# A rotary embedding on one core: every other row added on TensorE, VectorE makes a sine product in single batches, loads issued 18 rows behind

## The chip, the cores and the metric

The kernel runs on one core of a Trainium2 chip. A core has five engines, each with its own stream of instructions: TensorE (PE; its weight loads are shown as PEld), VectorE (DVE), ScalarE (ACT), GpSimd (POOL) and SyncE (SP). Transfers between the device's memory and the core's on-chip memory are done by sixteen DMA engines; they are issued here by ACT (loads) and SP (stores). The metric is the device time of one execution in microseconds, as a median over runs; less is better.

## What is computed

```python
batch, seq, dim = (16, 512, 1024); num_heads = 16; head_dim = 64
x = x.reshape(batch, seq, num_heads, head_dim)
x1, x2 = (x[..., :half_dim], x[..., half_dim:])
cos = cos[None, :, None, :]
sin = sin[None, :, None, :]
rotated = np.concatenate([x1 * cos - x2 * sin, x1 * sin + x2 * cos], axis=-1)
```

All in float32. 33.6 MB are read and 33.6 MB written. For each element there are two products (one with the cosine; one of the other half of its head with the sine, negative for the first half) and one add.

## The kernel before

**Tiles and rows.** The 128 partitions hold the sequence. Batches 0, 1, 14 and 15 are loaded one at a time (R1 = 4 positions of the sequence per partition), the others in six pairs (R2 = 8 positions). That makes ten tiles: two singles, six pairs, two singles. A "row" is one position per partition, 128 x 1024 floats (0.52 MB); there are NU = 64 rows, numbered through. `x_sb` is a ring of RING = 40 rows, worked on in place: the result of a row is written over its input and stored from there.

**Work on a row u.**

- a sine product into `t2_sb` (a ring of NT2 = 6 buffers, shown as t_sb in the profile): POOL (L257), or, where V2[u] is true, DVE (L286), with the halves of each head swapped as it reads and a signed sine table
- a cosine product into `t1_ps` (a ring of NT1 = 3 buffers in the accumulation memory, t_ps in the profile): always DVE (L293)
- the add. Where PE2[u] is false, DVE adds the two and writes `x_sb` (L304, `comb`). Where it is true, TensorE multiplies the sine product with an identity matrix and accumulates on the cosine product (L224, two 512-wide matmuls, seen as four records), and ACT copies the sum to `x_sb` (L191)

PE2 is true for rows 1, 3 and 6 of every eight, except in the first and the last batch: 21 rows. V2 is true for row 3 of every pair: six rows. Thus POOL makes 58 sine products.

**Order.** DVE goes through the rows: `mul(u)`, then `comb(u - 1)` if that row is not PE's. `mul(u)` waits until row u - 3 is added, by ACT's copy or DVE's add, because it takes over its buffer. POOL, and DVE where it makes the sine product, wait until row u - 6 is added. PE waits for both products of its row. ACT's stream holds the copies in order of rows and the loads among them.

**Tables.** The cosine and sine tables are loaded once, 64 KB each. ACT makes signed sine tables for POOL (L182 to L187). For its own sine product of pairs DVE makes a small signed table `v_ps` (L271, L272: 0.19 us each) just before row 8.

**Loads and stores.** The first six loads (tiles 0 to 5, 40 rows) are issued at once. Each of the other four takes over a place in the ring. It stands in ACT's stream behind the copies up to a certain row and waits there until the store of the rows whose place it takes has landed:

```python
later.setdefault((b * R1 - RING) // R2 * R2 + R2 - 1 + LAG, []).append(t)
```

With LAG = 10 the seventh load stands after row 17, the eighth after row 25, the ninth and tenth after row 33. SP issues the store of a tile when all its rows are added (L161).

Of the kernel before, what the change touches and what calls it, by code (L numbers as in the profile page):

```python
# [6 lines left out]
def bass_split_heads_rope_kernel(  # L7
# [18 lines left out]
    HD = dim // H  # L26
    HALF = HD // 2
    P = 128
    R1 = seq // P
    R2 = 2 * R1  # L30
# [4 lines left out]
    mult = mybir.AluOpType.mult  # L35
# [5 lines left out]
    tiles = [(b, R1 if b in singles else R2) for b in range(batch) if b in singles or b % 2 == 0]  # L41
    NT = len(tiles)
    RING = 5 * R2

    rows = [(t, r) for t, (_, n) in enumerate(tiles) for r in range(n)]
    NU = len(rows)
    EARLY = (NU - RING) // R2


    V_ROW = 3  # L50
    PE2 = [R1 <= u < NU - R1 and u % R2 in (1, 3, 6) for u in range(NU)]
    V2 = [tiles[t][1] == R2 and r == V_ROW for t, r in rows]

    def count(flags):
        return [sum(flags[: u + 1]) for u in range(NU)]

    n_pool = count([not v for v in V2])
    n_pe = count(PE2)
    n_comb = count([not a for a in PE2])

    NT1 = 3
    NT2 = 6
    BANK = 512
    EH = H * HD // BANK
    LEAD = 1
    LAG = 10

    with ExitStack() as stack:
        x_sb = stack.enter_context(nc.sbuf_tensor([P, RING, H, 2, HALF], fp32))
        t2_sb = stack.enter_context(nc.sbuf_tensor([P, NT2, H, 2, HALF], fp32))  # L70
        stage = stack.enter_context(nc.sbuf_tensor([P, 2, R1 * HALF], fp32))
# [5 lines left out]
        tab_ps = stack.enter_context(nc.psum_tensor([P, BANK], fp32))  # L77
        pair_ps = stack.enter_context(nc.psum_tensor([P, 2, 2, R1, HALF], fp32))
# [5 lines left out]
        sem_sin = stack.enter_context(nc.semaphore("sin"))  # L84
        sem_c = stack.enter_context(nc.semaphore("ctab"))
# [10 lines left out]
        sem_a = stack.enter_context(nc.semaphore("act"))  # L96

        c1_ps = tab_ps[:, 0:R1 * HALF].rearrange("p (r d) -> p r d", d=HALF)
        v_ps = tab_ps[:, R1 * HALF:R1 * HALF + HD].rearrange("p (t d) -> p t d", d=HALF)

        def c_of(t, r):
            return c1_ps[:, r, :] if tiles[t][1] == R1 else pair_ps[:, r // R1, 0, r % R1, :]
# [19 lines left out]
        def where(u):  # L122
            t, r = rows[u]
            return t, r, u % RING

        def swapped(k):
            return x_sb[:, k, :, ::-1, :]

        def over_heads(table):
            return table[:, None, :, :].broadcast_to([P, H, 2, HALF])  # L130
# [8 lines left out]
        def wait_t2_free(eng, u):  # L139

            if u >= NT2:
                v = u - NT2
                if PE2[v]:
                    eng.wait_ge(sem_e, n_pe[v])
                else:
                    eng.wait_ge(sem_v, n_comb[v])
# [17 lines left out]
        def on_scalar(ae):  # L164
            later = {}
            for t, (b, n) in enumerate(tiles):
                if b * R1 + n <= RING:
                    load(ae, t)
                else:

                    later.setdefault((b * R1 - RING) // R2 * R2 + R2 - 1 + LAG, []).append(t)
                if t == 0:
# [15 lines left out]
            for u in range(NU):  # L188
                if PE2[u]:
                    ae.wait_ge(sem_e, n_pe[u])  # L190
# [6 lines left out]
        def on_tensor(pe):  # L197
# [17 lines left out]
            for u in range(NU):  # L215
                if not PE2[u]:
                    continue
                pe.wait_ge(sem_m, u + 1)

                if not V2[u]:  # L220
                    pe.wait_ge(sem_p, n_pool[u])
# [12 lines left out]
        def on_gpsimd(pl):  # L234
# [11 lines left out]
            for u in range(NU):  # L246
                if V2[u]:
                    continue
# [12 lines left out]
        def on_vector(ve):  # L261
            ve.memset(zero[:], 0.0).then_inc(sem_z, 1)  # L262
            ve.wait_ge(sem_cos, 16)
            ve.tensor_copy(c1_ps, stage[:, 0, :].rearrange("s (r d) -> s r d", d=HALF)).then_inc(sem_c, 1)  # L264
            ve.wait_ge(sem_c, 1)
            ve.wait_ge(sem_w, NT1 * EH)

            def pair_tables():
                ve.wait_ge(sem_s, 2)
                row = pair_ps[:, V_ROW // R1, 1, V_ROW % R1, :]  # L270
                ve.tensor_scalar_mul(v_ps[:, 0, :], row, -1.0).then_inc(sem_c, 1)  # L271
                ve.tensor_copy(v_ps[:, 1, :], row).then_inc(sem_c, 1)  # L272

            first_v = V2.index(True)

            def mul(u):
                t, r, k = where(u)
                if r == 0:
                    ve.wait_ge(sem_in[t], 16)
                if (t, r) == (2, 0):  # L280
                    pair_tables()
                if u == first_v:
                    ve.wait_ge(sem_c, 3)
                if V2[u]:
                    wait_t2_free(ve, u)
                    ve.tensor_tensor(t2_sb[:, u % NT2, :, :, :], swapped(k), over_heads(v_ps), mult)  # L286
                if u >= NT1:
                    v = u - NT1
                    if PE2[v]:
                        ve.wait_ge(sem_a, n_pe[v])  # L290
                    else:
                        ve.wait_ge(sem_v, n_comb[v])
                ve.tensor_tensor(  # L293
                    t1_ps[:, u % NT1, :].rearrange("p (h d) -> p h d", d=HALF),
                    x_sb[:, k, :, :, :].rearrange("p h t d -> p (h t) d"),
                    c_of(t, r)[:, None, :].broadcast_to([P, 2 * H, HALF]),
                    mult,
                ).then_inc(sem_m, 1)

            def comb(u):  # L300
                t, r, k = where(u)
                ve.wait_ge(sem_m, u + 1)
                ve.wait_ge(sem_p, n_pool[u])  # L303
                ve.tensor_tensor(  # L304
                    xs[:, k, :],
                    t1_ps[:, u % NT1, :],
                    t2_sb[:, u % NT2, :, :, :].rearrange("p h t d -> p (h t d)"),
                    add,
                ).then_inc(sem_v, 1)

            for u in range(NU + LEAD):
                if u < NU:
                    mul(u)
                if u >= LEAD and not PE2[u - LEAD]:
                    comb(u - LEAD)
# [3 lines left out]
        on_gpsimd(nc.gpsimd)  # L319
        on_tensor(nc.tensor)  # L320
        on_vector(nc.vector)


# [31 lines left out]
```

## Time and profile before

| | |
|---|---|
| median of 3 runs | 161.54 us (161.3 to 161.56) |
| span of the profiled execution, first to last instruction | 160.3 us |
| POOL busy | 134.9 us (84%), 64 instructions |
| DVE busy | 130.3 us (81%), 117 instructions |
| PE busy | 72.8 us (45%), 94 instructions |
| ACT busy | 24.4 us (15%), 27 instructions |
| DMA | 67.26 MB, mean 419 GB/s over the span |
| load issues (seventh to tenth) | 53.6, 73.6, 93.1, 93.4 us |
| store issues, first and last | 20.5, 151.7 us |

Busy time is the time in which an engine executes; issuing a DMA and waiting are not in it. The profiled execution's own device time is not listed apart from its span; the median of the runs is 1.2 us above that span. A row of forty digits shows busy tenths in forty slices of 4.0 us, 9 meaning 90% or more.

### The profile page before, as it was taken

How to read it: one execution, taken by the hardware profiler on the slowest of the kernel's cores; microseconds unless marked ns; L12 is line 12 of the kernel's file. 1: busy time of each engine (PE TensorE's matmuls, PEld its weight loads, DVE VectorE, ACT ScalarE, POOL GpSimd, SP SyncE). 2: the span in 40 equal slices, each digit the busy share in tenths (PEclk: the TensorE clock that was granted, in tenths of full speed). 3: DMA queues.
4: the chain of work that ended last, by engine and by line, in shares of the span. 5: the costliest groups of instructions: out<-in, count | busy, mean ns of one | idle time of the engine just before them, and what ended most of it. 6: DMA issues, size and time to landing. Idle time of an engine off the chain costs nothing.

```text
span 160.3 us, 522 instructions
## 1 busy us (share of the span) xinstructions
PE 72.8 (45%) x94; PEld 24.0 (15%) x94; DVE 130.3 (81%) x117; ACT 24.4 (15%) x27; POOL 134.9 (84%) x64
## 2 busy tenths in 40 slices
PE   6050004478357936660847105489458435850000
PEld 1020002022202211210221002022202111220000
DVE  0069998599989999996999709899889999999500
ACT  0420000203120222022012010201220402040000
POOL 1059999999999999999999999699999999289400
PEclk9955555557755587689687965555555977699555
DMA  5999999999999999999999999999999999999896
GB/s 147 409 441 474 409 450 409 425 429 429 446 429 458 417 411 466 409 433 401 450 433 425 425 409 458 409 433 433 411 429 462 441 417 401 450 441 441 376 450 294
DMA packets 3170, 67.26 MB, mean 419 GB/s; under 512 B 352, under 2 KB 608, under 8 KB 608
## 3 DMA queue, kind: packets, MB, share of 16 engines
q10 hardware_dynamic: 1728, 33.69, 49.6%
q1 hardware_dynamic: 1440, 33.56, 48.9%
q14 instruction: 2, 0.02, 0.0%
HBM read 33.69 MB, written 33.55 MB: 419 GB/s over the span
## 4 chain that ended last, share of the span: by engine, by line
DMA 60%; POOL 13%; DVE 8%; PE 7%; issue 3%; ACT 2%; ACTq 1%; DVEq 0%
DMA x_sb<-in_x_dram 41%; DMA out_dram<-x_sb 18%; POOL t_sb L257 13%; PE t_ps L224 7%; DVE t_ps L293 5%; DVE x_sb L304 3%; ACT x_sb L191 2%; ACTq L153 1%; ACTq L174 1%; DVE t_sb L286 0%; DVEq L303 0%
## 5 line engine op out<-in xcount | busy, mean ns | idle before, releaser
L257 POOL TENSOR_TENSOR t_sb<-x_sb,s_sb 128x1024 f32<-128x1024 f32 x58 | 134.2, 2346 | 14.8 <-ACT s_sb L183 8.5
L224 PE MATMUL t_ps<-t_sb,ident 128*128 128x512 f32 x84 | 68.0, 957 | 63.0 <-DVE t_ps L293 39.2
L293 DVE TENSOR_TENSOR t_ps<-x_sb,pair_ps 128x1024 f32<-128x1024 f32 x48 | 57.7, 1223 | 9.9 <-ACT x_sb L191 9.8
L304 DVE TENSOR_TENSOR x_sb<-t_ps,t_sb 128x1024 f32<-128x1024 f32 x43 | 52.4, 1218 | 2.6 <-POOL t_sb L257 2.6
L224 PEld LDWEIGHTS t_ps<-t_sb,ident 128*128 128x128 f32 x84 | 22.1, 290 | 108.9 <-DVE t_ps L293 74.6
L191 ACT ACTIVATE x_sb<-t_ps 128x1024 f32<-128x1024 f32 x21 | 21.5, 1023 | 109.9 <-PE t_ps L224 96.9
L293 DVE TENSOR_TENSOR t_ps<-x_sb,tab_ps 128x1024 f32<-128x1024 f32 x16 | 19.3, 1222 | 0.1
L286 DVE TENSOR_TENSOR t_sb<-x_sb,tab_ps 128x1024 f32<-128x1024 f32 x6 | 7.3, 1213 | 0.0
L264 DVE COPY tab_ps<-stage 128x128 f32<-128x128 f32 x1 | 0.3, 294 | 7.8 <-DMA stage<-in_cos_dram 7.8
L208 PE MATMUL pair_ps<-stage,pick 128*128 128x256 f32 x4 | 2.0, 667 | 5.4 <-DMA stage<-in_sin_dram 5.4
L201 PE MATMUL t_ps<-zero 128*128 128x512 bf16 x6 | 2.7, 627 | 1.3 <-DVE zero L262 1.3
L208 PEld LDWEIGHTS pair_ps<-stage,pick 128*128 128x128 f32 x4 | 1.2, 324 | 6.4 <-issue 6.3
L177 ACT ACT_TABLE_LOAD x1 | 1.3, 1283 | 5.5 <-issue 5.5
L201 PEld LDWEIGHTS t_ps<-zero 128*128 128x128 bf16 x6 | 0.7, 136 | 2.4 <-DVE zero L262 1.2
L262 DVE MEMSET zero<- 128x256 uint32 x1 | 0.3, 272 | 0.9 <-PEq L337 0.9
L186 ACT ACTIVATE s_sb<-pair_ps 128x256 f32<-128x256 f32 x1 | 0.4, 383 | 1.7 <-PE pair_ps L208 1.7
L182 ACT ACTIVATE s_sb<-stage 128x128 f32<-128x128 f32 x1 | 0.3, 309 | 2.1 <-DMA stage<-in_sin_dram 2.1
L235 POOL MEMSET ident<- 128x128 f32 x1 | 0.2, 204 | 0.3 <-POOLq L337 0.3
L177 ACT ACTIVATE pick<-ident 128x256 f32<-128x256 f32 x1 | 0.4, 416 | 0.0
L187 ACT ACTIVATE s_sb<-pair_ps 128x256 f32<-128x256 f32 x1 | 0.4, 379 | 0.0
L237 POOL TENSOR_SCALAR_AFFINE_SELECT ident<-ident 128x128 f32<-128x128 f32 x1 | 0.3, 292 | 0.1
L337 POOL MEMSET const-float32-0.0<- 128x1 f32 x1 | 0.1, 98 | 0.3 <-issue 0.3
(6 smaller groups left out, 1.0 us busy)
## 6 DMA issues: line engine op xcount, KB each, us to landing
x_sb<-in_x_dram ACTq DMA_DIRECT2D x6, 4096.0 KB, 38.0
out_dram<-x_sb SPq DMA_DIRECT2D x6, 4096.0 KB, 25.0
x_sb<-in_x_dram ACTq DMA_DIRECT2D x4, 2048.0 KB, 22.6
out_dram<-x_sb SPq DMA_DIRECT2D x4, 2048.0 KB, 15.2
stage<-in_cos_dram ACTq DMA_DIRECT2D x1, 64.0 KB, 7.8
stage<-in_sin_dram ACTq DMA_DIRECT2D x1, 64.0 KB, 7.5
```

Of the source, the lines that this page charges most:

```text
L153: eng.dma_start(in_sbuf(t), in_dram(x1, x2, t)).then_inc(sem_in[t], 16)
L174: ae.dma_start(stage[:, i, :], table.rearrange("(s r) d -> s (r d)", r=R1)).then_inc(sem, 16)
L177: ae.activation(pick[:], ident[:].rearrange("q (s k) -> q k s", k=2)[:, :, :, None].broadcast_to([P, 2, P // 2, 2]), COPY).then_inc(sem_g, 1)
L186: ae.activation(s2[:, :, :, 0, :], pair_ps[:, :, 1, :, :], COPY, scale=-1.0)
L191: ae.activation(xs[:, u % RING, :], t1_ps[:, u % NT1, :], COPY).then_inc(sem_a, 1)
L201: pe.matmul(t1_ps[:, k, b * BANK:(b + 1) * BANK], zero[:, 0:P], zero[:], start=True, stop=True).then_inc(sem_w, 1)
L208: pe.matmul(pair_ps[:, k].rearrange("p c r d -> p (c r d)"), pick[:, k].rearrange("q s b -> q (s b)"), stage[:].rearrange("q c f -> q (c f)"),
L224: ins = pe.matmul(t1_ps[:, u % NT1, b * BANK:(b + 1) * BANK], ident[:], t2[:, b * BANK:(b + 1) * BANK], start=False, stop=True, skip_group ...
L257: pl.tensor_tensor(t2_sb[:, u % NT2, :, :, :], swapped(k), over_heads(s_of(t, r)), mult).then_inc(sem_p, 1)
L286: ve.tensor_tensor(t2_sb[:, u % NT2, :, :, :], swapped(k), over_heads(v_ps), mult)
L293: ve.tensor_tensor(t1_ps[:, u % NT1, :].rearrange("p (h d) -> p h d", d=HALF), x_sb[:, k, :, :, :].rearrange("p h t d -> p (h t) d"), c_of ...
L304: ve.tensor_tensor(xs[:, k, :], t1_ps[:, u % NT1, :], t2_sb[:, u % NT2, :, :, :].rearrange("p h t d -> p (h t d)"), add,).then_inc(sem_v, 1)
```

## The change

The rows that TensorE adds are given by row of the tile: 1 and 3 in single batches, 1, 3, 5 and 7 in pairs, only row 1 in the last batch. DVE makes one sine product in single batches too (row 1), besides row 3 in pairs; it gets a second small table for that, made at its start from the loaded sine table. LAG goes from 10 to 18.

```diff
-    V_ROW = 3
-    PE2 = [R1 <= u < NU - R1 and u % R2 in (1, 3, 6) for u in range(NU)]
-    V2 = [tiles[t][1] == R2 and r == V_ROW for t, r in rows]
+    V_ROW = {R1: 1, R2: 3}
+    PE_ROWS = {R1: (1, 3), R2: (1, 3, 5, 7)}
+    PE2 = [r in PE_ROWS[tiles[t][1]] and (t < NT - 1 or r == V_ROW[R1]) for t, r in rows]
+    V2 = [r == V_ROW[tiles[t][1]] for t, r in rows]
...
-    LAG = 10
+    LAG = 18
...
-        v_ps = tab_ps[:, R1 * HALF:R1 * HALF + HD].rearrange("p (t d) -> p t d", d=HALF)
+        v_ps = {
+            n: tab_ps[:, R1 * HALF + i * HD:R1 * HALF + (i + 1) * HD].rearrange("p (t d) -> p t d", d=HALF)
+            for i, n in enumerate((R1, R2))
+        }
...
             ve.tensor_copy(c1_ps, stage[:, 0, :].rearrange("s (r d) -> s r d", d=HALF)).then_inc(sem_c, 1)
+
+            def v_table(n, row):
+                ve.tensor_scalar_mul(v_ps[n][:, 0, :], row, -1.0).then_inc(sem_c, 1)
+                ve.tensor_copy(v_ps[n][:, 1, :], row).then_inc(sem_c, 1)
+
+            ve.wait_ge(sem_sin, 16)
+            v_table(R1, stage[:, 1, V_ROW[R1] * HALF:(V_ROW[R1] + 1) * HALF])
             ve.wait_ge(sem_c, 1)
...
             def pair_tables():
                 ve.wait_ge(sem_s, 2)
-                row = pair_ps[:, V_ROW // R1, 1, V_ROW % R1, :]
-                ve.tensor_scalar_mul(v_ps[:, 0, :], row, -1.0).then_inc(sem_c, 1)
-                ve.tensor_copy(v_ps[:, 1, :], row).then_inc(sem_c, 1)
-
-            first_v = V2.index(True)
+                v = V_ROW[R2]
+                v_table(R2, pair_ps[:, v // R1, 1, v % R1, :])
+
+            made = {V2.index(True): 3, rows.index((2, V_ROW[R2])): 5}
...
-                if u == first_v:
-                    ve.wait_ge(sem_c, 3)
+                if u in made:
+                    ve.wait_ge(sem_c, made[u])
                 if V2[u]:
                     wait_t2_free(ve, u)
-                    ve.tensor_tensor(t2_sb[:, u % NT2, :, :, :], swapped(k), over_heads(v_ps), mult)
+                    ve.tensor_tensor(t2_sb[:, u % NT2, :, :, :], swapped(k), over_heads(v_ps[tiles[t][1]]), mult)
```

After it PE2 is true for 31 rows and V2 for ten; POOL makes 54 sine products. The seventh load stands in ACT's stream after row 25, the eighth after row 33, the ninth and tenth after row 41.

## The prediction

> **What bounds the kernel now.** I read the DMA rows of the page first, since everything that enters or leaves passes there.
>
> ```profile
> DMA  5999999999999999999999999999999999999896
> ...
> DMA packets 3170, 67.26 MB, mean 419 GB/s; under 512 B 352, under 2 KB 608, under 8 KB 608
> ...
> q10 hardware_dynamic: 1728, 33.69, 49.6%
> q1 hardware_dynamic: 1440, 33.56, 48.9%
> ```
>
> The reader is to see a row of nines. Packets of loads (q10) and stores (q1) take 49.6 + 48.9 = 98.5% of the sixteen engines' span: 157.9 of 160.3 us. The view by stretches says where the other 2.4 us lie (columns: length, busy time and count of PE, PEld, DVE, ACT, POOL, clock, DMA share, GB/s).
>
> ```profile
> 0.00:4.00 4.00, 2.74 (x6) 0.72 (x6) 0.27 (x1) 0.00 (x0) 0.70 (x6) 1.00 0.53 147
> 4.00:20.00 16.00, 2.05 (x4) 1.18 (x4) 10.35 (x10) 2.87 (x6) 10.15 (x5) 0.61 1.01 430
> 20.00:40.00 20.00, 10.22 (x12) 3.37 (x12) 17.67 (x18) 2.43 (x3) 20.00 (x10) 0.54 1.01 433
> ...
> 60.00:80.00 20.00, 11.45 (x16) 3.48 (x14) 18.46 (x18) 3.13 (x4) 20.00 (x10) 0.77 1.00 428
> ...
> 100.00:120.00 20.00, 12.99 (x14) 3.59 (x13) 18.77 (x18) 4.09 (x4) 17.69 (x8) 0.50 0.98 422
> ...
> 140.00:150.00 10.00, 2.36 (x5) 0.88 (x4) 9.32 (x9) 2.05 (x2) 8.98 (x4) 0.84 0.98 423
> ...
> 153.00:156.00 3.00, 0.00 (x0) 0.00 (x0) 0.00 (x0) 0.00 (x0) 0.00 (x0) 0.50 1.00 426
> 156.00:161.00 5.00, 0.00 (x0) 0.00 (x0) 0.00 (x0) 0.00 (x0) 0.00 (x0) 0.50 0.64 275
> ```
>
> The first 4 us lack 0.47 x 4 = 1.9 us of traffic, and the last stretch, cut at 160.3, holds 0.64 x 5 = 3.2 us in 4.3: 1.1 us missing. That is already more than 2.4, so nothing is idle between. Even at 153 to 156 us, with no compute engine working, the engines are full: stores are queued up.
>
> The chain of waits names others at the end, and must be read against that.
>
> ```profile
> 93.45 47.51 DMA x_sb<-in_x_dram
> 140.96 0.07 issue
> 141.02 9.29 POOL t_sb L257 x4
> ...
> 150.40 1.23 DVE x_sb L304
> ```
>
> The last load lands at 140.96, four POOL rows and an add follow, and the last store is issued at 151.70 by the row of the stores and lands 8.6 us later. Its 2,048 KB need only 2.10 MB / 430 GB/s = 4.9 us; the other 3.7 us are start-up and queueing behind the stores before it. The first load needed 1.9 - 0.8 = 1.1 us from issue to traffic, so the last store could have come up to 3.7 - 1.1 = 2.6 us later without leaving the engines idle. I count 1 to 2.6 us of slack.
>
> **The change part by part.** Durations are from these rows:
>
> ```profile
> L257 POOL TENSOR_TENSOR t_sb<-x_sb,s_sb 128x1024 f32<-128x1024 f32 x58 | 134.2, 2346 | 14.8 <-ACT s_sb L183 8.5
> L224 PE MATMUL t_ps<-t_sb,ident 128*128 128x512 f32 x84 | 68.0, 957 | 63.0 <-DVE t_ps L293 39.2
> L304 DVE TENSOR_TENSOR x_sb<-t_ps,t_sb 128x1024 f32<-128x1024 f32 x43 | 52.4, 1218 | 2.6 <-POOL t_sb L257 2.6
> L191 ACT ACTIVATE x_sb<-t_ps 128x1024 f32<-128x1024 f32 x21 | 21.5, 1023 | 109.9 <-PE t_ps L224 96.9
> ```
>
> *Adds.* PE rows go from 21 to 31: four in each of six pairs, two in three single batches, one in the last. DVE loses ten adds, ten copies move to ACT (10 x 1.02 us), and PE gains ten rows of up to 3.8 us (at clock 0.50 in the timeline; 2.0 us in its fastest rows). *Sine products.* Four rows leave POOL, 58 to 54: 4 x 2.33 = 9.3 us. DVE takes them at 1.13 us from start to start. DVE in all: -10 + 4 = -6 instructions, 6.8 us fewer. The new table costs two small instructions of 0.19 us (as L271 and L272) before DVE's first product, 9.37 to 9.75; POOL starts at 9.85 anyway. The new wait for the sine table costs nothing: ACT used it at 9.26, while DVE's cosine copy runs from 9.04 to 9.33.
>
> Pace per eight rows: POOL 7 x 2.33 = 16.3 in pairs, and now in singles also (before 18.6); DVE 13 x 1.13 = 14.7 (before 15.8); PE 4 x 3.78 = 15.1 when slow; ACT 4.1. POOL still sets it. DMA needs 2 x 4.19 MB / 430 = 19.5 us for the same rows. All compute time saved lies beside DMA and is worth nothing on the path.
>
> The new price not in the trace is the ring of three product buffers, where a PE row holds its buffer through POOL, PE and ACT. From below: the pace of 16.84 us between the ACT-released products at 96.58 and 113.42, with three slow PE rows. From above: a whole turn in series, 1.22 + 2.33 + 3.78 + 1.02 = 8.35 us per three rows, 22.3 per eight. I take 16.8: PE's row can begin as soon as POOL ends, and the next products were already written then (DVE waited for ACT only 9.8 us in all, 8 times, longest 5.3). The pace that would hurt: sixty rows must be through by 141, so (141 - 9.85) / 7.5 = 17.5 us per eight.
>
> The TensorE page of the Trainium skill (TensorE: Matmul & The Clock Gate, Part 1) says that idle windows halve the clock and about 3.4 us of sustained work restore it. Here rows took 3.78 us at 0.50 with 2.38 us idle before them. By the rule closer rows would run warm at about 2 us; by the row they stay at 3.78. The sum is the same, as POOL is slower than both.
>
> *Waits and stores.* DVE's sine product, with its cosine product and adds behind it, waits until the row six earlier is added; in pairs that is now a PE row. It has three rows' time, some 6 us, against 3.8; the nearest row is POOL's wait for PE, 2.0 us in two. I take 0. SP's stores of pairs now wait for a copy of row 7, behind PE: up to 3.8 + 1.0 - 1.2 = 3.6 us later each than an add by DVE. Stores queued before them hide it (a pair's store takes 25.0 us to land, 10 of them its own transfer).
>
> *Loads.* ACT issues them in its own order, so four issues at three places move past eight rows' copies each. Last in front of them is now the copy of row 25, 33, 41 (before 17, 25, 33). POOL has done 22, 29, 36 products by then (rows less those of DVE): 9.85 + 22 x 2.33 = 61.1, 77.4, 93.7; plus 3.78 and 1.02 and hand-offs: 66, 82, 98.6. Before they were issued at 53.6, 73.6, 93.1. A load costs nothing while the load queue has work. The sixth load was issued at 4.8 and took the longest, 67.5 us: it landed at 72.3. So the seventh, issued at 66, is 6 us ahead of a dry queue. It landed 36 to 38 us after 53.6, near 91; the eighth at 82 is 9 us ahead. POOL waited for that one until 111.39; the last two at 99, or 101 if row 40 waits for its data at 91, are 10 us ahead. Cost nothing: queued loads cover it. If that cover were gone, the last load would land later, then row 60, then the last store.
>
> The waits in the copies' queue go: the store of rows 8 to 15 held ACT to 73.6, the next to 93.1, and behind each stood a copy that freed a buffer for DVE:
>
> ```profile
> DVE t_ps L293 <- ACT x_sb L191: 9.8, 8, 5.3
> ...
> ACT x_sb L191 <- DMA out_dram<-x_sb: 4.2, 1, 4.2
> ```
>
> At 82 and 99 those stores have landed. DVE gains some 6 us, POOL some; both then wait for loads instead. The first store goes from 20.5 to 21.8 (three POOL rows to 16.8, PE 3.8, copy 1.0), under loads that fill the engines.
>
> The DMA page of the Trainium skill (DMA: Bandwidth & Descriptors, Rules for kernel authors) speaks against this: issue a transfer early and wait for it late. By the rule later issues cost; by the rows above none is late enough, because its queue is never empty.
>
> *End.* Last load near 141 as before, three POOL rows instead of four (7.0), add 1.3: last store at 149.4 instead of 151.7. It only waits longer behind other stores. Saving 0.
>
> Sum: 160.3 - 0 (adds) - 0 (products) + 0 (loads) - 0 (end) = 160.3 us of span. The median of the runs is 161.54, 1.2 above this span, so 161.5.
>
> **Rivals.** *A, smoother traffic.* Against the best stretches' 433 GB/s, the slower ones lack, over their lengths, 16 x 3 + 20 x 5 + 20 x 11 + 10 x 10 = 468 GB/s x us, which is 468 / 433 = 1.1 us. The issue at 73.6, after a store's landing, lies in one of them, so other interleaving of reads and writes may win part. Against: 20 to 60, also mixed, is at 433. Price 0 to 1.1; half: 161.0.
>
> *B, rougher traffic.* The same mechanism turned round: loads and stores now meet at other places. From the same bounds +0.6: 162.1.
>
> *C, a pace above what DMA covers; the slower side.* If a PE row holds its buffer long enough, DVE waits for ACT at every turn and the ring sets the pace; a quarter of the way from 16.8 to 22.3 it is 18.2. Sixty rows are then through (18.2 - 17.5) x 7.5 = 5.2 us after 141, the last store goes out at 149.4 + 5.2 = 154.6 where 152.7 to 154.3 is still covered: 0.3 to 1.9 late, say 1.2, so 162.7. The loads feel it at the same place: row 25's copy, 66 at pace 16.3, moves by 3.2 x 1.9 = 6.1 to 72, where the queue runs dry. It decides from about 17.8 on; each 0.1 above costs 0.75 us, and at 22.3 the kernel would be far outside any range given here. For it: DVE already waits for ACT with three PE rows. Against: 15.1 of PE against 16.3 of POOL, and a DVE with less to do.
>
> **How the numbers follow.** About 0.2% (0.32 us) is what a measurement can tell from no change. Forecast, DMA bound as before: 0.54, of it 0.48 within that limit and 0.03 on each side. A 0.24, B 0.10, C 0.12. Faster 0.24 + 0.03 = 0.27, same 0.48, slower 0.10 + 0.12 + 0.03 = 0.25. The forecast alone spans 161.2 to 161.9. The range goes down to 160.7, past A's half price, and up to 162.8, over B and about half of C: some 0.06 is left out below and 0.08 above.
>
> **What would show it.** Right: DMA row of nines to the last slices; queues' shares still near 98.5%; load issues near 66, 82 and 99; no wait of ACT for a store; POOL waiting longer for loads; last load landing at 139 to 142, last store issued near 149.4 yet landing at about 160. Wrong: products that wait for ACT at each turn and a last store after 154 (C), or stretches whose rate differs by 10 GB/s with full engines (A or B). The forecast also fails if a load queue runs dry near 70, 91 or 111 with no stores waiting.

## The result, and the profile after

| | before | after |
|---|---|---|
| median of 9 runs | 161.3 us (161.08 to 161.56) | 162.02 us (161.57 to 162.99) |
| ratio | | 1.0049, 95% interval 1.0029 to 1.007 |
| profiled execution: span | 160.3 us | 160.4 us (its run: 161.69) |

The changed kernel is 0.5% slower, outside what measurement leaves open, and its runs scatter over 1.4 us where before they scattered over 0.5. The spans of its nine runs go from 160.3 to 161.7 us; the profiled one is among the shortest, so the profile shows the cause and not its usual size. Ratios here and below leave out disturbed runs (the page shown for e7 is of one) and are not always the quotient of the medians beside them.

These are the DMA rows of the page of the changed kernel:

```profile
DMA  5999999999999999999999999999999999999895
...
DMA packets 3171, 67.27 MB, mean 419 GB/s; under 512 B 352, under 2 KB 608, under 8 KB 608
...
q10 hardware_dynamic: 1728, 33.69, 49.5%
q1 hardware_dynamic: 1440, 33.56, 48.7%
q8 instruction: 1, 0.02, 0.0%
q14 instruction: 2, 0.02, 0.0%
```

The row of nines is still there, and loads and stores still fill 98.2% of the engines' span. The last slice has 5 instead of 6. And there is one packet more, 3,171 for 3,170, on a queue q8 that the page of before does not list: a fetch of instructions, 16,384 bytes. (q14 holds two fetches of 8,192 bytes in both kernels.)

The chain of waits of the changed kernel near its end, and its groups (line, engine, names, shapes, count | busy us, mean ns | idle time and who ended it):

```profile
64.42 27.57 DMA x_sb<-in_x_dram
...
101.03 40.05 DMA x_sb<-in_x_dram
141.08 0.02 issue
141.10 1.23 DVE t_ps L303
...
149.03 1.22 DVE x_sb L314
```

```profile
L261 POOL TENSOR_TENSOR t_sb<-x_sb,s_sb 128x1024 f32<-128x1024 f32 x54 | 125.1, 2362 | 21.6 <-DMA x_sb<-in_x_dram 13.2
L228 PE MATMUL t_ps<-t_sb,ident 128*128 128x512 f32 x124 | 79.3, 784 | 58.0 <-POOL t_sb L261 32.7
L195 ACT ACTIVATE x_sb<-t_ps 128x1024 f32<-128x1024 f32 x31 | 31.8, 1024 | 105.9 <-PE t_ps L228 105.9
```

Nothing here is worse. The last load lands at 141.08 (before 140.96). POOL now waits 13.2 us for loads, before 4.3: it has time to spare. ACT waits for PE alone; its wait for a store's landing is gone. The last store is issued at 150.32, 1.4 us earlier than before, and still the kernel ends no earlier.

The view by stretches of the last 2 us shows why the earlier issue gained nothing (the last two columns are DMA share and GB/s). It counts a packet with its whole time in the stretch in which it starts, so that a share can be above 1, and a low one means that few packets start. First the kernel before:

```profile
158.50:159.00 0.50, 0.00 (x0) 0.00 (x0) 0.00 (x0) 0.00 (x0) 0.00 (x0) 0.50 0.54 229
159.00:159.50 0.50, 0.00 (x0) 0.00 (x0) 0.00 (x0) 0.00 (x0) 0.00 (x0) 0.50 0.69 295
```

Then the changed kernel:

```profile
157.00:158.50 1.50, 0.00 (x0) 0.00 (x0) 0.00 (x0) 0.00 (x0) 0.00 (x0) 0.50 0.87 371
158.50:159.00 0.50, 0.00 (x0) 0.00 (x0) 0.00 (x0) 0.00 (x0) 0.00 (x0) 0.50 0.62 262
159.00:159.50 0.50, 0.00 (x0) 0.00 (x0) 0.00 (x0) 0.00 (x0) 0.00 (x0) 0.50 0.09 33
```

Between 159.0 and 159.5 nine packets of 16 KB still start before, and one after (0.09). When the engines stop is said by the ends of the packets. Every store closes with sixteen packets of 4 bytes, after 128 of 32 KB (a pair) or of 16 KB (a single batch); I take this as sixteen equal parts, one for each DMA engine. Before, the parts of the last store end between 158.74 and 159.94, the last two 0.03 apart. After, seven end at 158.55 to 158.63, eight at 159.11 to 159.49, and one at 160.03. A store ends with the engine that has most to do, and only one has the fetch.

The packets of the trace say what the fetch costs the engine that carries it. In the stretch around it (queue, kind: packets, MB, share of the sixteen engines' 1.2 us):

```profile
q1 hardware_dynamic: 11, 0.36, 70.2%
q10 hardware_dynamic: 16, 0.26, 53.5%
q8 instruction: 1, 0.02, 4.8%
```

4.8% of 16 x 1.2 us is 0.92 us. The fetch starts at 121.02 and takes 0.93, and a 16 KB load packet starting at 121.94, as it ends, takes 1.107 us where most take 0.611. Together 0.93 + 0.50 = 1.43 us of one engine.

The trace does not number the engines, but it lets one be followed. Its next packet starts 3 or 4 ns before the last one ends (14 ns after the fetch). From the fetch on there is at every step only one packet that fits (queue, start and end in us, ns, bytes):

```
q8   121.019  121.950   931  16384   the fetch
q10  121.936  123.043  1107  16384
q1   123.039  124.253  1214  32768
...
q1   159.414  160.025   611  16384
q1   160.021  160.030     9      4   closes the last store
```

These are 52 packets without a pause, and they end at 160.03: the engine that carried the fetch is the one that ends last. Only the first two took longer than usual.

The end of each store on the last and on the second last of the sixteen engines follows from the closing packets. For five of the last six stores of some executions, those of the experiments below among them (us, second last to last):

```
before            111.34-111.78  125.96-126.42  140.51-140.54  ...  155.05-155.08  159.91-159.94   no fetch
after             110.89-111.00  125.54-126.08  140.08-140.62  ...  154.63-155.17  159.49-160.03   fetch at 121.0
e1_before_pad     111.04-111.36  125.99-126.30  139.93-140.84  ...  154.47-155.39  159.33-160.25   fetch at 113.9
e3_after_lag10    110.70-111.08  125.88-127.34  140.70-141.88  ...  155.24-156.43  160.11-161.29   fetch at 122.3
e5_pad_early      110.92-111.61  125.50-126.16  139.98-140.70  ...  154.52-155.24  159.38-160.11   fetch at 61.8
e8_pad_250        111.64-111.75  126.26-126.29  140.98-141.47  ...  155.53-156.02  160.39-160.88   fetch at 135.2
e2_after_lean     110.61-110.77  125.15-125.31  139.69-139.86  ...  154.24-154.40  159.10-159.26   no fetch
e4_before_lag18   111.38-111.78  126.53-126.92  141.07-141.47  ...  156.23-156.62  161.09-161.49   no fetch
```

After the change the two are 0.11 apart in the store before the fetch and 0.54 in every store after it. Such a gap by itself does not prove a fetch: before has 0.46 at 126 us, which is gone at 140, e1 has 1.02 in its first store, long before its fetch, and e7's page, without this fetch, ends with 1.87. What ties gap and fetch together is the chain of packets. Followed in the same way, the engine with the fetch is the one that ends last in all five executions with one fetch, without a pause and with one candidate at every step. In the last store it ends 0.49 to 1.18 us after the next engine; in before, e2 and e4, without a fetch, the gap is 0.03 to 0.40.

This also gives the price. The fetch and the slower packet behind it cost their engine 1.43 to 1.50 us in each of the five. Without them, all else being the same, it would have ended at 158.60 (after), 158.75 (e1), 159.86 (e3), 158.68 (e5) and 159.45 (e8), each time before the engine that is now second last. So the kernel loses the 1.4 to 1.5 us less what that engine was early: 0.54, 0.92, 1.18, 0.73 and 0.49 us.

### The profile page after: what moved, and what is told of

It reads as the page before. It is cut to its first block, busy times and chain, and to the rows that moved or that the text cites. A ratio compares the mean times of both kernels' runs of the same rounds, so it can differ in the third digit from the quotient of the medians.

```text
span 160.4 us, 601 instructions
## 1 busy us (share of the span) xinstructions
PE 84.1 (52%) x134; PEld 29.6 (18%) x134; DVE 123.7 (77%) x113; ACT 34.6 (22%) x37; POOL 125.8 (78%) x60
## 2 busy tenths in 40 slices
DMA packets 3171, 67.27 MB, mean 419 GB/s; under 512 B 352, under 2 KB 608, under 8 KB 608
## 4 chain that ended last, share of the span: by engine, by line
DMA 54%; POOL 26%; PE 5%; DVE 4%; issue 3%; ACTq 1%; ACT 0%
DMA x_sb<-in_x_dram 54%; POOL t_sb L261 26%; PE t_ps L228 5%; DVE t_ps L303 2%; DVE x_sb L314 2%; DVE t_sb L296 1%; ACTq L157 1%; ACTq L178 1%; ACT x_sb L195 0%
## 5 line engine op out<-in xcount | busy, mean ns | idle before, releaser
L261 POOL TENSOR_TENSOR t_sb<-x_sb,s_sb 128x1024 f32<-128x1024 f32 x54 | 125.1, 2362 | 21.6 <-DMA x_sb<-in_x_dram 13.2
L228 PE MATMUL t_ps<-t_sb,ident 128*128 128x512 f32 x124 | 79.3, 784 | 58.0 <-POOL t_sb L261 32.7
L303 DVE TENSOR_TENSOR t_ps<-x_sb,pair_ps 128x1024 f32<-128x1024 f32 x48 | 57.1, 1223 | 11.5 <-DMA x_sb<-in_x_dram 6.1
L195 ACT ACTIVATE x_sb<-t_ps 128x1024 f32<-128x1024 f32 x31 | 31.8, 1024 | 105.9 <-PE t_ps L228 105.9
L228 PEld LDWEIGHTS t_ps<-t_sb,ident 128*128 128x128 f32 x124 | 27.7, 244 | 108.7 <-issue 55.7
L314 DVE TENSOR_TENSOR x_sb<-t_ps,t_sb 128x1024 f32<-128x1024 f32 x33 | 40.2, 1220 | 1.0 <-POOL t_sb L261 0.6
L296 DVE TENSOR_TENSOR t_sb<-x_sb,tab_ps 128x1024 f32<-128x1024 f32 x10 | 12.1, 1215 | 0.0
```

Source lines behind the costliest of these rows:

```text
L195: ae.activation(xs[:, u % RING, :], t1_ps[:, u % NT1, :], COPY).then_inc(sem_a, 1)
L228: ins = pe.matmul(t1_ps[:, u % NT1, b * BANK:(b + 1) * BANK], ident[:], t2[:, b * BANK:(b + 1) * BANK], start=False, stop=True, skip_group ...
L261: pl.tensor_tensor(t2_sb[:, u % NT2, :, :, :], swapped(k), over_heads(s_of(t, r)), mult).then_inc(sem_p, 1)
L303: ve.tensor_tensor(t1_ps[:, u % NT1, :].rearrange("p (h d) -> p h d", d=HALF), x_sb[:, k, :, :, :].rearrange("p h t d -> p (h t) d"), c_of ...
L314: ve.tensor_tensor(xs[:, k, :], t1_ps[:, u % NT1, :], t2_sb[:, u % NT2, :, :, :].rearrange("p h t d -> p (h t d)"), add,).then_inc(sem_v, 1)
```

## The experiments

The fetch suggested a theory: TensorE's stream of instructions became longer (206 in the trace before, 292 after; a row costs it eight records, four weight loads and four matmuls, and some waits), so that it needs one more fetch, and that is the loss (theory 1). The rivals: the later loads (theory 2), or the rows on TensorE and the new meeting of reads and writes (theory 3; the latter is rival B of the prediction).

**e1: a longer TensorE stream alone.** In the kernel before:

```diff
+                for _ in range(8):
+                    pe.wait_ge(sem_z, 1)
                 pe.wait_ge(sem_m, u + 1)
```

Two such waits make one instruction of the trace (168 waits, 84 instructions).

> The kernel before with 84 more instructions in TensorE's stream (four per row that it adds, each a wait for something long done), so that the stream has 290 instructions, about as many as after the change (292), and nothing else. Theory 1 (the longer stream of TensorE is fetched by one more 16 KB transfer, seen at 121.0 us after the change and not before; it takes 0.93 us of one DMA engine, and that engine ends its share of the last store later): the transfer appears, one of the sixteen last-store ends stands 0.5 us or more apart, the time is 0.3 to 1.2 us above before and the runs scatter more than before's 161.1 to 161.6. Theory 2 (later loads cost): no change, within 0.2%. Theory 3 (more rows on TensorE or the order of reads and writes costs): no change.

161.96 us, ratio 1.0049 (1.0034 to 1.0064): the loss of the whole change, from a kernel whose arithmetic, loads and stores are those of before. The DMA rows of its page:

```profile
DMA packets 3171, 67.27 MB, mean 419 GB/s; under 512 B 352, under 2 KB 608, under 8 KB 608
...
q8 instruction: 1, 0.02, 0.0%
```

The extra packet is here too, at 113.9 us, 0.94 us long. One engine ends the last store at 160.25, the next at 159.33, and the first is the one that carried the fetch. So theory 1 holds and theories 2 and 3 cannot explain this run. A fourth would be that the added waits slow TensorE itself; no run has such waits without a fetch. The last store was indeed issued later, at 152.19 instead of 151.70, but the engine that ended last had worked without a pause since 113.9, and the other fifteen ended earlier than before (159.33 against 159.94).

**e2: the change with a short stream.** In the changed kernel:

```diff
-    PE_ROWS = {R1: (1, 3), R2: (1, 3, 5, 7)}
-    PE2 = [r in PE_ROWS[tiles[t][1]] and (t < NT - 1 or r == V_ROW[R1]) for t, r in rows]
+    PE_ROWS = {R1: (1, 3), R2: (1, 3, 6)}
+    PE2 = [r in PE_ROWS[tiles[t][1]] and t < NT - 1 for t, r in rows]
```

> The changed kernel with TensorE adding rows 1, 3, 6 of pairs and none of the last batch: 24 rows instead of 31, some 230 instructions in TensorE's stream; LAG 18 and the sine products of single batches stay. Theory 1: no 16 KB transfer, time 0.3 to 1.0 us below the changed kernel, 161.0 to 161.6. Theory 2: as slow as the changed kernel, 161.8 to 162.2. Theory 3: between the two.

161.49 us, ratio 1.001 (0.9993 to 1.0027): not to be told from before. Its page lists no q8:

```profile
DMA packets 3170, 67.26 MB, mean 421 GB/s; under 512 B 352, under 2 KB 608, under 8 KB 608
...
q10 hardware_dynamic: 1728, 33.69, 49.8%
q1 hardware_dynamic: 1440, 33.56, 48.9%
q14 instruction: 2, 0.02, 0.0%
```

LAG 18 and the sine products of single batches are still in it, so within the interval these cost nothing together, and gain nothing either. It also has seven rows fewer on TensorE; by itself it could not tell the fetch from the rows, but e1 has the fetch without any more rows.

**e3 and e4: LAG alone.** The changed kernel with LAG = 10, and the kernel before with LAG = 18.

> The changed kernel with LAG back at 10. Theory 1: the 16 KB transfer stays, the time stays near 162.0 and scatters. Theory 2: back at the time before, 161.3. Theory 3: as the changed kernel.

> The kernel before with LAG 18 alone. Theory 1: no 16 KB transfer and the time before, at most 0.8 us more from a load queue that runs dry for a moment near 70 us, as compute is slower here than with the other parts. Theory 2: 0.5 to 1 us slower. Theory 3: no change.

e3: 161.91 us, ratio 1.0063 (1.0035 to 1.009), with the fetch at 122.3: as slow as the changed kernel, so LAG is not what cost the time there. e4: 162.69 us, ratio 1.0087 (1.0074 to 1.01), with no fetch: a loss of another kind, and larger than either theory allowed (1.4 us of median). The chain of e4 and the stretches of its end:

```profile
104.23 39.43 DMA x_sb<-in_x_dram
143.65 0.07 issue
143.72 9.28 POOL t_sb L257 x4
...
153.09 1.22 DVE x_sb L304
```

```profile
153.00:154.00 1.00, 0.00 (x0) 0.00 (x0) 0.91 (x1) 0.00 (x0) 0.00 (x0) 0.50 1.15 492
154.00:155.00 1.00, 0.00 (x0) 0.00 (x0) 0.32 (x1) 0.00 (x0) 0.00 (x0) 0.50 0.54 229
155.00:156.00 1.00, 0.00 (x0) 0.00 (x0) 0.00 (x0) 0.00 (x0) 0.00 (x0) 0.50 1.11 475
```

The last load lands 2.7 us later than in the kernel before, the last store goes out at 154.39 instead of 151.70, and at 154 to 155 few packets start: the stores queued before it have run out on some engines. Packet by packet, some 0.35 us of all engines' time is empty between 154.3 and 155.5. So later loads do cost with the compute of before. In the changed kernel the same LAG has faster compute to cover it (last load at 141.1, last store at 150.3), and costs nothing.

Where the 2.7 us begin can be read from the loads. In e4 the seventh was issued at 68.76. The sixteen parts of the sixth ended between 71.32 and 72.20, but the first packet of the seventh started only at 73.42, 4.7 us after its issue. It landed at 95.18 instead of 91.87, and the loads after it kept that delay. So the load queue did run dry, though the seventh was issued 3.4 us ahead of the sixth's end. In the changed kernel it was issued at 64.42, and its first packet followed the sixth's at 71.33. Load packets of e4 also took 1.3 to 2.1 us instead of 1.21 near 74 and 90 us; why was not settled.

**e5: when the fetch falls.** In the kernel before, 170 instructions more in TensorE's stream where it waits for its first tables and its first row:

```diff
+            for _ in range(80):
+                pe.wait_ge(sem_z, 1)
             pe.wait_ge(sem_g, 1)
...
                 ).then_inc(sem_t, 1)
+            for _ in range(260):
+                pe.wait_ge(sem_z, 1)
             for u in range(NU):
```

> The kernel before with 170 more instructions in TensorE's stream (376 in all), all of them in the first 26 us, where TensorE waits anyway, so that the fetch falls near 26 us and not near 115. Theory 1 (a fixed extra amount of work on one of sixteen engines that share every transfer equally): where the fetch falls does not matter, one last-store end stands apart, 161.8 to 162.2, as e1. Rival (the fetch hurts because it is late, when the last rows and stores have no slack): back at the time before, 161.3.

162.22 us, ratio 1.0038 (1.002 to 1.0056). The fetch came at 61.8 us, not at 26 as meant: it starts when 254 of TensorE's instructions have started, 216 to 249 in the other four executions, and the padding was too little for that by 26 us. Still it is some 50 us earlier than 113.9 in e1. The interval overlaps that of e1: no recovery is seen, though nearly 100 us remain after the fetch. The engine with the fetch could be followed through 110 packets to the end, where it is the last. That fits an engine with a fixed share, and speaks against a loss at the end alone.

**e6: two fetches.** e5's padding and, before each row of TensorE, eight instructions as in e1 (544 in all).

> The kernel before with 338 more instructions in TensorE's stream (544 in all), enough for two fetches. Theory 1: two 16 KB transfers; if the same DMA engine carries both, the last-store end of that engine stands twice as far apart and the time is near 162.8 (twice the 0.7 of e1 above 161.3); if two engines carry one each, the time is that of e1, near 162.0. Rival (TensorE stalls while its instructions arrive): TensorE's rows begin later after each fetch and the last store is issued later than 152.5.

162.26 us, ratio 1.0062 (1.0039 to 1.0084). Two packets on q8, at 30.2 and 120.4 us. The last store ends at 161.24 on one engine, 160.16 on the next and 159.41 on the third: two stand apart, which points to two engines carrying one each. Here two engines ran too close together to be followed. The interval overlaps that of e1, so whether a second fetch adds anything stays open. Its last store was issued at 153.03, later than the rival's mark of 152.5. The parts of the store before it ended between 153.74 and 156.38, so at most the earliest engines ran short; the run does not exclude that TensorE lost some time.

**e7: another engine's stream.** In the kernel before, ScalarE's stream gets 160 instructions before its first copy and four after each copy, again waits for something long done.

> The kernel before with 244 more instructions in ScalarE's stream (285 in all), nothing more in TensorE's. If any engine's stream beyond some 250 instructions is fetched by such transfers, one or more appear and the time is 161.6 to 162.2. If it is TensorE's alone, no transfer and 161.3, within 0.2%.

161.38 us, ratio 1.0001 (0.9988 to 1.0015): no loss. Its page has no q8, but two more fetches on q14:

```profile
DMA packets 3172, 67.27 MB, mean 414 GB/s; under 512 B 352, under 2 KB 608, under 8 KB 608
...
q14 instruction: 4, 0.03, 0.0%
```

These are of 8,192 bytes and 0.309 us each. So ScalarE's stream is fetched as well, in smaller pieces, and what two of these cost is within the interval. The expectation had "one or more appear and the time is 161.6 to 162.2": two appeared, but smaller and on another queue, and the time did not rise.

**e8: where it begins.** e1 with `range(4)`: 248 instructions.

> The kernel before with 42 more instructions in TensorE's stream, 248 in all: where the transfer begins to be needed. 230 instructions (e2) had none, 290 had one. If it appears here, the limit lies at or below 248 and the time is near 162.0; if not, it lies between 248 and 290 and the time is 161.3.

162.41 us, ratio 1.0061 (1.0042 to 1.0081), one packet on q8, at 135.2 us. Counted in instructions of the trace, the limit lies above 230 (e2) and at or below 248.

No run was faster than the kernel before by more than its interval; e2, the best of the versions with the change in it, equals it.

## Why the prediction was wrong

The time, 162.02, lay inside the range given, but the kernel became slower, to which the prediction gave 0.25, and none of the rivals named the cause. That 162.02 lies beside rival B's 162.1 is luck: the upper part of the range was drawn for B and C, and it was neither.

- *What bounds the kernel* was right: full DMA engines, before and after. All compute time saved was worth nothing.
- *Adds* is the step that failed: the sum has "0 (adds)", with no cost either, and the ten rows were priced as time of TensorE, DVE and ACT alone. They are also 86 more instructions in one stream (206 to 292), and between 230 and 248 these bring a 16 KB transfer onto the resource that was full. Measured by itself (e1) the term is +0.65 us of median, ratio 1.0049; the prediction had 0. On the profile of before one could have seen a row "q14 instruction", that is, that code comes over the same engines, though not its price.
- The slack was counted for the sum of sixteen engines. The end is that of the slowest: in the profiled execution fifteen stopped by 159.49 and one at 160.03.
- *Loads* was right in place and price: issues at 64.4, 81.2 and 100.7 us (66, 82, 99 to 101 expected), last landing at 141.1, and nothing lost (e2; e3 against the changed kernel). The margin was mis-sized: the seventh load was held to be 6 us ahead of a dry queue, counted from its issue, but in e4 it needed 4.7 us from issue to its first packet, and an issue 2.8 us later than 66 already found the queue dry. What the prediction says follows then (the last load later, then the last store) is what e4 did, for 0.87%.
- *End*: the last store was expected at 149.4 and came at 150.32, as two of DVE's adds stand in a row from 147.90 (POOL's last product ends at 148.12), where one was counted. *First store*: 19.76 instead of 21.8; TensorE's second row of it took 1.96 us and not 3.78.
- *Ring*: DVE's wait for ACT fell from 9.8 to 5.8 us; rival C did not come about. The two ways of pricing TensorE rows gave the same sum, and closer rows did run faster: 784 ns a matmul instead of 957, at a mean clock of 0.816 instead of 0.662. That closer rows run warmer is what the Trainium skill's page TensorE: Matmul & The Clock Gate, Part 1, would have; its 3.4 us were not tested here.
- *A and B*, smoother or rougher traffic: by the prediction's own mark of 10 GB/s three stretches do differ (60 to 80 us: 428 before, 439 after; 100 to 120: 422 and 434; 140 to 150: 423 and 411), in both directions. They add up to nothing that can be told: e2, with much the same interleaving and no fetch, equals before.

The Trainium skill has the mechanism: Runtime: NRT & Kernel Launch, Instruction fetch mechanics, says that an engine's instructions come in 16 KiB blocks of 256 by DMA, and that crossing such a boundary is "mostly hidden". The runs agree with the block for TensorE (16,384 bytes, a limit between 230 and 248 seen instructions), not for ScalarE (8,192 bytes, e7), and differ on the cost: with all sixteen engines full it was 0.49% (e1).

## What to carry to other kernels

When the DMA engines are full from start to end, anything else that travels on them can lengthen the kernel, by what it costs its engine less what that engine was early (here 1.43 to 1.50 us, of which 0.49 to 1.18 were lost): look at instruction fetches in the queue list, and count the instructions that an edit adds to each stream, not only their time. Work moved from one engine to another is not free because both have idle time; here TensorE was 45% busy. And a transfer issued later is free only as long as it is issued well before its queue runs dry, 3.4 us being too little here: LAG 18 cost nothing with faster compute and 0.87% without.

## What the runs showed of the hardware

- TensorE's stream was fetched in one piece of 16,384 bytes on a queue of its own, once 248 or more instructions were in it (none with 230); a fetch took 0.88 to 1.06 us on its DMA engine, against 0.611 for most data packets of the same size, and where the engine could be followed the packet behind it took 0.49 to 0.56 us more than usual. ScalarE's longer stream brought two pieces of 8,192 bytes on q14, 0.309 us each.
- The fetch made runs scatter: 161.57 to 162.99 us after the change, 161.08 to 161.56 before, beside e1 161.13 to 161.76 before and 161.78 to 162.51 in e1. In the five executions that were followed the loss was 0.49 to 1.18 us, by how early the engine with the fetch was. For the other runs, of which no packets are on record, this is not shown, and the longest span after the change, 161.7, is above the 159.49 + 1.43 = 160.9 that the profiled execution would allow.
- A load issued behind a full load queue had its first packet 4.7 us after its issue in e4, when the queue had meanwhile run dry for 1.2 us (72.20 to 73.42).
